# Making the two parts of 48 weight tiles with a casting transfer, a ScalarE multiplication and an adding transfer

## The chip, the cores and the metric

The kernel runs on one core of one Trainium2 chip. The metric is the device time of one execution in microseconds (us); lower is better. The kernel before was timed three times: 2293.43, 2293.59 and 2295.14 us, median 2293.59.

## What is computed

Four layers of a small language model run one after the other on 512 tokens of width 1024, all in float32: a gated linear recurrence, an attention with forget gates, and twice a hybrid layer (the "second block"). Only the hybrid layer's short convolution is touched by the change. Cut to that, the reference is:

```python
def hybrid_layer(x, positions, ...):
    h = rmsnorm(x, norm_mix)
    proj = h @ w_in                                  # w_in: 1024 x 9216
    cb, cc, cu, q, k, v, g, ga, gb = jnp.split(proj, split_points, axis=-1)
    z = conv(cc * cu)                                # depthwise, 3 taps
    y_conv = (cb * z) @ w_conv_out
    y_ret = retention_mixer(q, k, v, g, ...)
    merged = jax.nn.sigmoid(ga) * y_conv + jax.nn.sigmoid(gb) * y_ret
    x = x + merged @ w_o
    h2 = rmsnorm(x, norm_mlp)
    return x + jnp.square(jax.nn.relu(h2 @ w_up)) @ w_down
```

cb, cc and cu are 1024 wide each, so each layer has 3 x 8 output tiles of 128 features, and the two layers have 48.

## The kernel before

Activations lie with features on the 128 partitions and the 512 tokens along the free side. Every matrix product is done three times on parts of its operands: a float32 value is split into a high part in TensorE's reduced format (float32r) and a low part that holds the rest, and the products high x high, high x low and low x high are added up in PSUM. These are the three matmuls of `mm3`, lines 254, 255 and 256. One projection, `proj`, takes one weight tile of 128 x 1024 (eight blocks of 128 x 128) through 24 matmuls on 512 columns and gives one output tile of 128 features.

The class `Stream` makes the weight tiles in the order of their use. For each it loads the raw tile on SP's queue (512 KB), lets ScalarE cast it into the high part `wh` (line 59) and VectorE subtract that from the raw tile into the low part `wl` (line 60). Raw tiles have four buffers, high and low parts three each. A call of `next` sets going the work on tiles up to two ahead. As there are three buffers, tile i+3 can be written only when the last matmul that reads tile i is over: line 255 is the last reader of `wh`, line 256 that of `wl`.

In the convolution stage of a layer the loop runs over eight output tiles j. For each j it projects cb, cc and cu in this order (`cb_0`, `cc_0`, `cu_0`, `cb_1` and so on); VectorE empties each PSUM tile (lines 1089, 1092, 1095), applies the taps (1096, 1098), multiplies (1099), and splits the outcome into `zH` and `zL` with ScalarE (269, 270). GpSimd does little there: `rr`, the square of the row factor (1080), and two small fills (1085). The stage before it multiplies by `w_ret_out` (tiles `wr_0` to `wr_7`), the one behind it projects the gates `ga`.

TensorE's order is that of the program. The other engines' order is set by a scheduler that runs over the whole program; each engine and each queue then goes through its list strictly in order, and waits where an operand or a buffer isn't ready.

Of the kernel before, what the change touches and what calls it, by code (L numbers as in the profile page):

```python
# [7 lines left out]
F32 = mybir.dt.float32  # L8
F32R = mybir.dt.float32r
# [20 lines left out]

# columns of the packed per-partition vectors
VEC = {}
# [15 lines left out]
class Stream:  # L48
    """Weights in order of use: load, split into two float32r parts that add up exactly."""

    def __init__(self, tc, raw, hi, lo, items, ahead):
        self.nc, self.raw, self.hi, self.lo = tc.nc, raw, hi, lo
        self.items, self.ahead = items, ahead
        self.done, self.taken = [], 0
        self.sums = self.sraw = None
        self.pooled = 0  # so many of the next sums go to GpSimd, while VectorE has much else to do

# [4 lines left out]
    def _emit_sums(self, i, s1, s2):  # L62
        """Weights of two output tiles in Winograd's seven forms, each a pair of [P, 4, P] parts.

        Rows of the 2 x 2 blocks A are the output tiles, columns the halves of the contraction.
        """
        nc, hw, nh = self.nc, KD * P, KD * P // 2
        eng = nc.gpsimd if self.pooled > 0 else nc.vector
        self.pooled -= 1
        r1 = self.raw.tile([P, hw], F32, tag="wraw", name=f"wr{i}a")  # L70
        r2 = self.raw.tile([P, hw], F32, tag="wraw", name=f"wr{i}b")
        nc.sync.dma_start(r1, s1)
        nc.sync.dma_start(r2, s2)
        a11, a12, a21, a22 = r1[:, :nh], r1[:, nh:], r2[:, :nh], r2[:, nh:]
        out = {}

        def whole(names, src):
            h = self.hi.tile([P, hw], F32R, tag="whi", name=f"wh{i}{names[0]}")
            l = self.lo.tile([P, hw], F32R, tag="wlo", name=f"wl{i}{names[0]}")
            self._split(h, l, src)  # L80
            for n, nm in enumerate(names):
                c = slice(n * nh, (n + 1) * nh)
                out[nm] = tuple(t[:, c].rearrange("p (a b) -> p a b", b=P) for t in (h, l))

        def half(nm, src):
            h = self.sums.tile([P, nh], F32R, tag="shi", name=f"sh{i}{nm}")
            l = self.sums.tile([P, nh], F32R, tag="slo", name=f"sl{i}{nm}")
            self._split(h, l, src)
            out[nm] = tuple(t.rearrange("p (a b) -> p a b", b=P) for t in (h, l))

        def sraw(nm):
            return self.sraw.tile([P, nh], F32, tag="sraw", name=f"sr{i}{nm}")

        whole(("A11", "A12"), r1)
        v1 = sraw("S1")
        eng.tensor_add(v1, a21, a22)
        half("S1", v1)
        eng.tensor_sub(a21, a11, a21)
        whole(("S3", "A22"), r2)
        v2 = sraw("S2")  # L100
        eng.tensor_sub(v2, v1, a11)
        half("S2", v2)
        v4 = sraw("S4")
        eng.tensor_sub(v4, a12, v2)
        half("S4", v4)
        self.done.append(out)

    def _emit(self):
        nc = self.nc
        src, a, b = self.items[len(self.done)]  # L110
        if a is None:
            return self._emit_sums(len(self.done), src, b)
        n = a * b
        i = len(self.done)
        r = self.raw.tile([P, KD * P], F32, tag="wraw", name=f"wr{i}")
        h = self.hi.tile([P, KD * P], F32R, tag="whi", name=f"wh{i}")
        l = self.lo.tile([P, KD * P], F32R, tag="wlo", name=f"wl{i}")
        for c in range(0, n, n if i else n // 4):
            cs = slice(c, c + (n if i else n // 4))
            nc.sync.dma_start(r[:, cs], src[:, cs])  # L120
            self._split(h[:, cs], l[:, cs], r[:, cs])
        self.done.append(
            (h[:, :n].rearrange("p (a b) -> p a b", a=a), l[:, :n].rearrange("p (a b) -> p a b", a=a))
        )
# [16 lines left out]
class Map:  # L141
    """A pool whose tags stand for tags of other pools."""

# [8 lines left out]
def build(tc, A, out, dbg=None):  # L152
# [3 lines left out]
    with ctx:  # L156
# [11 lines left out]

# [1 line left out]
        items = []  # L170

# [30 lines left out]
        for l in range(2):  # L202
# [11 lines left out]
            for j in range(8):  # L214
                for t in range(3):
                    add(f"w_in{l}", 8 * t + j, KD, P)
            add(f"w_in{l}", 48, KD, P)
# [6 lines left out]
            for g in range(4):  # L224
                for f in range(0, 8, 2):
                    items.append((A[f"w_up{l}"][8 * g + f], None, A[f"w_up{l}"][8 * g + f + 1]))
                for j in range(8):
                    add(f"w_down{l}", 8 * g + j, KD, P)
        W = Stream(tc, wraw, whi, wlo, items, 2)

# [1 line left out]
        vec = cst.tile([P, NVEC], F32, name="vec")  # L232
# [38 lines left out]

# [1 line left out]
        def rsqrt_row(dst, src, scale, tp, tag, load=True):  # L273
            """dst = 1 / sqrt(src * scale + EPS), all float32 of one shape: a first value and a Newton step."""
            shape = [P, src.shape[-1]]
# [11 lines left out]
        def colsum(acc, tp, tag):  # L287
            """Sum of acc over its partitions, on every partition of a PSUM tile."""
            h = tp.tile([P, S], F32R, tag="cs_h", name=f"csh_{tag}")
# [7 lines left out]
        class Norm:  # L297
            """Splits x * gain as tiles of x come, and sums their squares."""

# [38 lines left out]
        class PairNorm:  # L338
            """As Norm, with Winograd's forms of x * gain: blocks are halves of the features by halves of the tokens."""

# [26 lines left out]
        def pair(tag, forms, cp, cs, first=False):  # L367
            """Two output tiles [P, S] by Winograd's variant of Strassen's product."""
            w = W.next()
# [47 lines left out]
        def columns(r, tag):  # L417
            """[P, 4]: the row r with tokens on partitions."""
            ps = psum(f"rc_{tag}")
# [6 lines left out]
        def log1p_small(dst, e, tp, shape, tag):  # L426
            """log(1 + e) for e in [0, 1], to float32 accuracy in relative terms."""
            d = tp.tile(shape, F32, tag="lp_d", name=f"lpd_{tag}")
# [14 lines left out]
        def trig():  # L443
            """cos and sin of position * frequency, [frequency twice, token]: sin on partitions ..63, cos on 64.. first."""
            pos, kk, ang = sind.bitcast(I32), sind, cosd
# [21 lines left out]
            act.copy(cosd[:64], cosd[64:])  # L467
            # rows 64.. multiply the second half into the first one
            act.mul(sind[64:], sind[:64], -1.0)

        # =====================================================================
        # layer 1: LRU
        # =====================================================================
        with ExitStack() as lc:
# [12 lines left out]

            # softplus(-a_param), times -4 and -8
            sp = cst.tile([P, 12], F32, name="sp")
# [130 lines left out]

        # =====================================================================
        # layer 2: forgetting attention
        # =====================================================================
        with ExitStack() as lc:
# [19 lines left out]

            # keys: high parts twice; low parts, and over the other half of the rows the cumulated forget gates
            k1 = t1.tile([P, 2, S], F32R, name="k1")
# [4 lines left out]
            def fox_forget(ft):  # L651
                """Log sigmoid of the forget gates, [token, block of tokens and head], in two parts."""
                fa, fe = (t2.tile([P, 64], F32, tag="pr1", name=n) for n in ("fa", "fe"))
# [17 lines left out]

            # P^T of a head, key block kb from column 384 * kb + query on
            PTW = 3 * 384 + S
# [185 lines left out]

        # =====================================================================  # L860
        # second block
        # =====================================================================
        def finish(ah, nrm, tp):
            """Last output tiles by halves of the tokens, with the last norm of one half beside the products of the other."""
            S2, JS = S // 2, (5, 6, 7)
# [58 lines left out]
        for li in range(2):  # L924
# [3 lines left out]
            with ExitStack() as lc:  # L928
# [24 lines left out]
                def first_rows():  # L953
                    """1 / rms of the layer's input, and what follows from it."""
                    if li:
                        r = nrm.rows(tn)
                    else:
                        # final norm of the first block and first norm of the second, in one
                        r0 = nrm.rows(tn)
# [221 lines left out]

# [1 line left out]
def lay_out(inputs):  # L1183
# [98 lines left out]
```

## Time and profile before

| | |
|---|---|
| median of three runs | 2293.59 us |
| profiled execution, span from first to last instruction | 2293.6 us |
| TensorE matmuls, busy | 2238.3 us, 98% |
| VectorE, busy | 1543.9 us, 67% |
| ScalarE, busy | 1065.4 us, 46% |
| GpSimd, busy | 369.0 us, 16% |
| moved by DMA | 210.42 MB, 92 GB/s on average |
| mean granted TensorE clock | 0.991 |

The profiled execution has no other time on its page than its span, which equals the median of the runs. Matmul durations overlap in the profile, since they are pipelined; how fast they follow one another is read from their starts. Line numbers in this part are those of the kernel before. In the changed kernel the code from `mm3` on stands 14 lines further down, and the cast and subtraction of `Stream` stand in lines 60 and 61.

### The profile page before, as it was taken

What the parts mean: (1) busy time and instruction counts of PE and PEld (TensorE: products, weight loads), DVE (VectorE), ACT (ScalarE), POOL (GpSimd) and SP (SyncE); (2) the same over time, 40 slices, a digit from 0 to 9 for tenths busy, and PEclk for the clock granted to TensorE, in tenths of its full rate; (3) what the DMA queues carried; (4) which work ended last, traced back from release to release, by engine and by line L of the source; (5) the groups of instructions that cost most, each with busy time, mean ns of one, the idle gap of its engine ahead of it and who ended that gap; (6) DMA issues with size and microseconds to landing.
All of it is one profiled execution on the core that took longest, in us unless ns stands there. A gap on an engine that the chain in (4) does not pass through costs nothing.

```text
span 2293.6 us, 30071 instructions
## 1 busy us (share of the span) xinstructions
PE 2238.3 (98%) x11818; PEld 1909.7 (83%) x11818; DVE 1543.9 (67%) x2256; ACT 1065.4 (46%) x1629; POOL 369.0 (16%) x269
## 2 busy tenths in 40 slices
PE   8898999999999999999999999999999999999998
PEld 6687778887888888887998998988888887998996
DVE  7987877777776445448875774766345548875774
ACT  5666577765556222235543444556222225443443
POOL 3434211113211000003310112211000004210112
PEclk9999999999999999999999999999999999999999
DMA  4133222222222332332332333222333322333331
GB/s 153 64 99 97 90 65 74 65 74 80 81 94 74 101 100 94 98 95 74 110 102 95 100 109 99 89 89 80 96 97 95 98 92 83 101 103 100 97 107 55
DMA packets 62509, 210.42 MB, mean 92 GB/s; under 512 B 6944, under 2 KB 11424, under 8 KB 62368
## 3 DMA queue, kind: packets, MB, share of 16 engines
q1 hardware_dynamic: 59552, 204.43, 28.1%
q10 hardware_dynamic: 2672, 3.81, 0.6%
q8 instruction: 93, 1.52, 0.3%
q14 instruction: 48, 0.39, 0.1%
q0 software_dynamic: 144, 0.26, 0.0%
HBM read 206.37 MB, written 2.10 MB: 91 GB/s over the span
## 4 chain that ended last, share of the span: by engine, by line
PE 82%; DVE 5%; ACT 1%; issue 1%; POOL 0%; DVEq 0%; ACTq 0%; POOLq 0%
PE dn L255 5%; PE dn L256 5%; PE dn L254 5%; PE up L255 4%; PE up L256 4%; PE up L254 4%; PE ro L981 1%; PE wr L256 1%; PE wc L254 1%; PE wc L256 1%; PE wc L255 1%; PE wr L255 1%; PE wr L254 1%; PE ga L254 1%; PE ga L256 1%
## 5 line engine op out<-in xcount | busy, mean ns | idle before, releaser
L59 ACT CAST wh<-wr 128x1024 fp32r<-128x1024 f32 (+2 forms) x332 | 337.2, 1017 | 707.9 <-PE dn L255 120.5
L60 DVE TENSOR_TENSOR wl<-wr,wh 128x1024 fp32r<-128x1024 f32 (+2 forms) x332 | 398.5, 1202 | 49.7 <-ACT wh L59 47.9
L255 PE MATMUL dn<-aL,wh 128*128 128x512 f32 x488 | 192.9, 395 | 0.3 <-DVE aL L270 0.3
L256 PE MATMUL dn<-aH,wl 128*128 128x512 f32 x488 | 192.8, 395 | 0.0
L254 PE MATMUL dn<-aH,wh 128*128 128x512 f32 x488 | 192.7, 395 | 0.0
L399 POOL TENSOR_TENSOR s_up<-s_up,sz_up 128x256 f32<-128x256 f32 x32 | 52.6, 1644 | 473.5 <-DVE sz_up L398 163.8
L1169 DVE TENSOR_TENSOR x<-dn,x 128x512 f32<-128x512 f32 x61 | 42.0, 689 | 111.1 <-PE dn L256 110.8
L255 PEld LDWEIGHTS dn<-aL,wh 128*128 128x128 f32 x488 | 91.5, 187 | 22.7 <-DVE aL L270 0.7
L256 PEld LDWEIGHTS dn<-aH,wl 128*128 128x128 f32 x488 | 91.5, 187 | 22.3
L254 PEld LDWEIGHTS dn<-aH,wh 128*128 128x128 f32 x488 | 91.5, 187 | 22.1
L326 POOL TENSOR_TENSOR nacc_m<-nacc_m,nsq_m 128x512 f32<-128x512 f32 x14 | 21.0, 1499 | 486.4 <-ACT nsq_m L325 486.4
L256 PE MATMUL rv<-wh,xL 128*128 128x256 f32 x256 | 72.4, 283 | 0.0
L255 PE MATMUL rv<-wl,xH 128*128 128x256 f32 x256 | 72.4, 283 | 0.0
L254 PE MATMUL rv<-wh,xH 128*128 128x256 f32 x256 | 72.4, 283 | 0.0
L1151 ACT ACTIVATE c_up<-c_up 128x512 f32<-128x512 f32 x64 | 40.5, 633 | 35.0 <-DVE c_up L1150 34.7
L254 PE MATMUL wo<-mH,wh 128*128 128x512 f32 x128 | 51.1, 399 | 0.0
L256 PE MATMUL wr<-yrH,wl 128*128 128x512 f32 x128 | 51.1, 399 | 0.0
L254 PE MATMUL wc<-zH,wh 128*128 128x512 f32 x128 | 50.6, 396 | 0.0
L256 PE MATMUL wc<-zH,wl 128*128 128x512 f32 x128 | 50.6, 395 | 0.0
L255 PE MATMUL wc<-zL,wh 128*128 128x512 f32 x128 | 50.5, 395 | 0.0
L255 PE MATMUL wr<-yrL,wh 128*128 128x512 f32 x128 | 50.5, 394 | 0.0
L256 PE MATMUL wo<-mH,wl 128*128 128x512 f32 x128 | 50.4, 394 | 0.0
(1561 smaller groups left out, 7144.5 us busy)
## 6 DMA issues: line engine op xcount, KB each, us to landing
wr<-in_w_in SPq DMA_DIRECT2D x112, 512.0 KB, 3.5
wr<-in_w_down SPq DMA_DIRECT2D x64, 512.0 KB, 3.5
wr<-in_fox_w_in SPq DMA_DIRECT2D x24, 512.0 KB, 3.5
wr<-in_lru_w_in SPq DMA_DIRECT2D x23, 512.0 KB, 3.6
wr<-in_w_v SPq DMA_DIRECT2D x16, 512.0 KB, 3.5
wr<-in_w_ret_out SPq DMA_DIRECT2D x16, 512.0 KB, 3.5
wr<-in_w_conv_out SPq DMA_DIRECT2D x16, 512.0 KB, 3.6
wr<-in_w_o SPq DMA_DIRECT2D x16, 512.0 KB, 3.5
```

What stands on the lines that cost most here:

```text
L59: self.nc.scalar.copy(h, src)
L60: self.nc.vector.tensor_sub(l, src, h.bitcast(F32))
L254: pe.matmul(ps, wH, aH, start=start, stop=False)
L255: pe.matmul(ps, wH, aL, start=False, stop=False)
L256: pe.matmul(ps, wL, aH, start=False, stop=stop)
L326: (dve if j > 5 and acc is self.acc2 else pool).tensor_add(acc, acc, sq)
L399: pool.tensor_add(s5, s5, z)
L981: pe.matmul(po[i][:, q0:], vp[:, kb, vs], sp_[:, so], start=n == 0, stop=n == 11)
L1151: act.activation(t, t, AF.Square)
L1169: dve.tensor_add(x[:, j], ps, x[:, j])
```

## The change

The 48 weight tiles of cb, cc and cu (24 in each layer) are made in another way; all others stay as they were. A set `by_dma` holds their places in the order of weights. For these, a transfer on GpSimd's queue casts the weights from memory straight into `wh`; ScalarE writes -`wh` into `wl`; and a second transfer on GpSimd's queue, with addition, adds the weights from memory to `wl`. The raw tile, its load on SP's queue and VectorE's subtraction fall away for them. Each of these weight tiles is read from memory twice.

```diff
@@ class Stream, _emit
         n = a * b
         i = len(self.done)
+        if i in self.by_dma:
+
+            h = self.hi.tile([P, KD * P], F32R, tag="whi", name=f"wh{i}")
+            l = self.lo.tile([P, KD * P], F32R, tag="wlo", name=f"wl{i}")
+            nc.gpsimd.dma_start(h[:, :n], src)
+            nc.scalar.mul(l[:, :n], h[:, :n].bitcast(F32), -1.0)
+            nc.gpsimd.dma_start(l[:, :n], src, accum_op=mybir.AluOpType.add)
+            self.done.append(
+                (h[:, :n].rearrange("p (a b) -> p a b", a=a), l[:, :n].rearrange("p (a b) -> p a b", a=a))
+            )
+            return
         r = self.raw.tile([P, KD * P], F32, tag="wraw", name=f"wr{i}")
@@ build
             for j in range(8):
                 for t in range(3):
+                    by_dma.add(len(items))
                     add(f"w_in{l}", 8 * t + j, KD, P)
...
         W = Stream(tc, wraw, whi, wlo, items, 2)
+        W.by_dma = by_dma
```

The rest of the diff takes comments out. TensorE's list is the same as before. In the lists below, `wh129` is the high part of weight tile 129, `wl129` its low part; tiles 129, 130, 131 are those of cb_0, cc_0, cu_0 of the first layer, 132 to 134 those of cb_1, cc_1, cu_1, and so on. In brackets stand the engines and queues that an instruction waits for (DMASW: GpSimd's transfers, DMAHW: those of the other queues).

GpSimd's list of the kernel before, from the last sum of the retention heads over the convolution stage to the first sum of squares behind it:

```order
L986 TENSOR_TENSOR gacc0_3_6664<-gacc0_3_6664,gsq0_3_6665 128x512 [waits DVE_49,Activation_49]
L1080 TENSOR_TENSOR rr_7201<-r_b_5201 128x512 [waits DMAHW5_49,DMAHW3_49,DMAHW6_49,DVE_49,DMAHW7_49,PE_49,Pool_49]
L1085 MEMSET zp0_7205 128x2
L1085 MEMSET zp1_7206 128x2
L326 TENSOR_TENSOR nacc_m0_8597<-nacc_m0_8597,nsq_m0_4_8676 128x512 [waits Activation_49]
```

There were three instructions in the whole stage. GpSimd's list of the changed kernel from the same place, where the stage begins:

```order
L1000 TENSOR_TENSOR gacc0_3_6664<-gacc0_3_6664,gsq0_3_6665 128x512 [waits DVE_49,Activation_49]
L120 DMA wh129_7126<-in_w_in0 128x1024 [waits DVE_49,PE_49]
L122 DMA wl129_7127<-in_w_in0 128x1024 [waits Activation_49]
L120 DMA wh130_7157<-in_w_in0 128x1024 [waits DVE_49,PE_49]
L122 DMA wl130_7158<-in_w_in0 128x1024 [waits Activation_49]
L120 DMA wh131_7208<-in_w_in0 128x1024 [waits DVE_49,PE_49]
L1094 TENSOR_TENSOR rr_7199<-r_b_5201 128x512 [waits DMAHW5_49,DMAHW6_49,DMAHW3_49,DMAHW7_49,PE_49,Pool_49]
```

Five transfers now stand between the heads' last sum and `rr`. The same list some rows further on, for the tiles of cb_1 to cc_2:

```order
L120 DMA wh132_7240<-in_w_in0 128x1024 [waits DMASW1_49,PE_49]
L122 DMA wl131_7209<-in_w_in0 128x1024 [waits Activation_49]
L122 DMA wl132_7241<-in_w_in0 128x1024 [waits DMASW2_49,Activation_49]
L120 DMA wh133_7272<-in_w_in0 128x1024 [waits DMASW3_49,PE_49]
L122 DMA wl133_7273<-in_w_in0 128x1024 [waits DMASW4_49,Activation_49]
L120 DMA wh134_7309<-in_w_in0 128x1024 [waits DMASW5_49,PE_49]
L120 DMA wh135_7341<-in_w_in0 128x1024 [waits DMASW6_49,PE_49]
L122 DMA wl134_7310<-in_w_in0 128x1024 [waits DMASW7_49,Activation_49]
L122 DMA wl135_7342<-in_w_in0 128x1024 [waits DMASW0_49,Activation_49]
L120 DMA wh136_7373<-in_w_in0 128x1024 [waits DMASW1_49,PE_49]
L122 DMA wl136_7374<-in_w_in0 128x1024 [waits DMASW2_49,Activation_49]
```

From here on a pattern of six rows repeats to the end of the stage: the casting transfers of a cu tile and of the cb tile behind it (134, 135), their two adding transfers, then the casting and the adding transfer of a cc tile (136). The adding transfer of a cu tile (`wl134`) has moved behind the casting transfer of the next cb tile (`wh135`), which waits for TensorE to give a buffer free. `wl131`, of cu_0, stands behind `wh132` in the same way.

## Rows read from the trace of the kernel before

**Rows 1.** The page: busy time by engine, and the chain by engine.

```profile
PE 2238.3 (98%) x11818; PEld 1909.7 (83%) x11818; DVE 1543.9 (67%) x2256; ACT 1065.4 (46%) x1629; POOL 369.0 (16%) x269
...
PE 82%; DVE 5%; ACT 1%; issue 1%; POOL 0%; DVEq 0%; ACTq 0%; POOLq 0%
```

**Rows 2.** Busy time by windows: the conv projections of both layers.

```profile
core 0: us, PE busy (x) PEld busy (x) DVE busy (x) ACT busy (x) POOL busy (x), PEclk, DMA share, GB/s
811.70:942.20 130.50, 130.50 (x577) 108.08 (x576) 67.22 (x83) 29.66 (x31) 1.11 (x3) 1.00 0.30 97
1675.40:1805.00 129.60, 129.60 (x573) 107.33 (x572) 69.53 (x87) 29.44 (x31) 0.00 (x0) 1.00 0.31 96
```

**Rows 3.** Tiles cb and cc: evacuations, min/median/max ns, first to last start.

```profile
L1089 DVE TENSOR_TENSOR cb<-cb,r_b x8: 691/692/692, 817.4 to 931.6; 128x512 f32<-128x512 f32 x8
...
L1092 DVE TENSOR_TENSOR cc<-cc,rr x16: 691/692/692, 822.9 to 1795.1; 128x512 f32<-128x512 f32 x16
```

**Rows 4.** Timeline of ScalarE, 811 to 823: start, length, idle before and releaser.

```profile
811.66 1.05 ACT L59 CAST wh<-wr 128x1024 fp32r<-128x1024 f32 x1 [4.55 <-PE wr L255]
...
822.59 1.06 ACT L59 CAST wh<-wr 128x1024 fp32r<-128x1024 f32 x1 [4.38 <-PE cc L255]
```

**Rows 5.** Timeline of all engines where the stage begins.

```profile
811.70 0.40 PE L254 MATMUL cb<-xH,wh 128*128 128x512 f32 x1
...
811.93 0.19 PEld L256 LDWEIGHTS cb<-xH,wl 128*128 128x128 f32 x1
...
812.00 1.04 POOL L1080 TENSOR_TENSOR rr<-r_b 128x512 f32<-128x512 f32 x1 [81.54 <-PE wr L256]
```

**Rows 6.** Groups by line in that window: busy us, mean ns, idle before.

```profile
L60 DVE TENSOR_TENSOR wl<-wr,wh 128x1024 fp32r<-128x1024 f32 x24 | 29.5, 1227 | 1.9 <-ACT wh L59 1.8
L59 ACT CAST wh<-wr 128x1024 fp32r<-128x1024 f32 x24 | 25.4, 1056 | 75.3 <-PE cc L255 35.1 <-PE cu L255 30.7 <-PE wr L255 4.6
```

**Rows 7.** DMA queues (packets, MB, share) and issues (KB each, us to landing).

```profile
q1 hardware_dynamic: 59552, 204.43, 28.1%
...
q0 software_dynamic: 144, 0.26, 0.0%
...
wr<-in_w_in SPq DMA_DIRECT2D x112, 512.0 KB, 3.5
...
wr<-in_fox_vf SPq DMA_DIRECT2D x1, 272.0 KB, 2.7
...
tri<-in_tri POOLq DMA_DIRECT2D x1, 256.0 KB, 3.2
```

**Rows 8.** Timeline of GpSimd around its one transfer.

```profile
263.51 0.74 POOL L643 DMA_DIRECT2D tri<-in_tri  x1 [0.31 <-POOL nacc_n L326]
264.30 0.52 POOL L648 MEMSET k<- 64x512 f32 x1
```

**Rows 9.** Timeline of TensorE where it idled: in brackets the idle time before.

```profile
289.85 0.74 PE L666 MATMUL cum<-tri,fH 128*16 128x512 f32 x4 [1.06 <-issue]
...
596.09 0.50 PE L254 MATMUL rs<-rqH,rkH 128*128 128x512 f32 x1 [1.57 <-ACT rkH L269]
```

**Rows 10.** Windows behind these, TensorE alone: length, busy, granted clock, DMA share, GB/s.

```profile
core 0: us, PE busy (x), PEclk, DMA share, GB/s
596.96:600.37 3.41, 3.41 (x12) 0.50 0.21 70
287.00:292.00 5.00, 3.94 (x21) 1.00 0.36 108
```

**Rows 11.** Timeline of TensorE at the lower clock.

```profile
564.06 0.63 PE L254 MATMUL rk<-xH,wh 128*128 128x512 f32 x1
564.49 0.63 PE L255 MATMUL rk<-xL,wh 128*128 128x512 f32 x1
564.91 0.63 PE L256 MATMUL rk<-xH,wl 128*128 128x512 f32 x1
```

**Rows 12.** Timeline of TensorE in the stage before.

```profile
807.96 0.40 PE L256 MATMUL wr<-yrH,wl 128*128 128x512 f32 x1
808.20 0.39 PE L254 MATMUL wr<-yrH,wh 128*128 128x512 f32 x1
808.43 0.39 PE L255 MATMUL wr<-yrL,wh 128*128 128x512 f32 x1
808.66 0.40 PE L256 MATMUL wr<-yrH,wl 128*128 128x512 f32 x1
```

More of the change, by code (lines that the diff above doesn't have):

```diff
@@ L55, in __init__ @@
         self.sums = self.sraw = None
+        self.by_dma = set()
         self.pooled = 0
@@ L167, in psum @@
             return psp.tile([P, S], F32, tag="ps", name=name)
-        items = []
+        items, by_dma = [], set()
         def add(name, idx, a, b):
```

## The prediction

> **What bounds the kernel now.** I read the busy table first: TensorE is busy 98% of the span, VectorE 67%, and the chain that ended last lies 82% on TensorE [rows 1]. The change touches 48 weight tiles, in one stage that comes twice (the projections cb, cc, cu of the two layers of the second block), so I then read the stage by windows: TensorE is busy 130.50 of 130.50 us in the first and 129.60 of 129.60 in the second [rows 2]. It waits for nothing there. VectorE works 67 of 130 us off the path; taking work from it can give nothing back in this stage. So the question is only whether the new way of making a weight tile is always done in time.
>
> Three distances decide that. One projection (24 matmuls on one weight tile): the evacuations of cb run from 817.4 to 931.6 us for eight outputs [rows 3], 114.2 us over 21 projections, 5.44 us each. When a buffer comes free: a pool holds three tiles, so tile i+3 goes where tile i was; before, ScalarE's cast starts at 811.66, 822.59 and so on, each time as the last L255 matmul of an older tile ends [rows 4]. From that event the next tile's low part is wanted 0.27 us later, by the weight load at 811.93 [rows 5]. Today the raw tile has long been loaded by then, and cast and subtraction take 1.06 + 1.23 us [rows 6] of two projections' 10.9 us.
>
> **The change part by part.** Removed in each stage: 24 loads on SP's queue, 24 casts (1.06 us) and 24 subtractions (29.5 us of VectorE) [rows 6]: worth 0, since TensorE waits for none of them. Added on ScalarE: 24 multiplications of the casts' shape. I take the cast's 1.06 us; no row has this one, but ScalarE is busy only 29.66 of 130.5 us [rows 2], so double would be hidden as well. The two zp fills and rr on GpSimd now stand behind a load; rr ran at 812.00 [rows 5] and its first reader is the evacuation of cc at 822.9 [rows 3]: nothing. SP's later loads start earlier, into raw buffers that the 48 tiles no longer use: nothing.
>
> What counts is the new chain, per tile: buffer free, casting load on GpSimd's queue, multiplication, adding load on the same queue. GpSimd takes its instructions in order, and the new order puts the adding load of each cu tile behind the casting load of the next cb tile, which waits until the projection two ahead of that cu has ended (the order is shown with the change). So cu's adding load has one projection, 5.44 us, plus the 0.27: 5.71 us.
>
> Prices. A casting load: the one that the trace has on GpSimd's queue, 256 KB, took 0.74 us to issue [rows 8] and 3.2 to land; on SP's queue 272 KB took 2.7 and 512 KB 3.5 [rows 7], so 512 KB cast is 3.2 + 0.85 = 4.05 us. How much of that is data: SP's queue moved 204.43 MB in 28.1% of 16 engines' span [rows 7], 0.281 x 2293.6 = 644.5 us with all 16, or 644.5 x 0.524 / 204.43 = 1.65 us per tile. Lead-in and landing are the other 2.4.
>
> An adding load is nowhere in the trace. Low end: it costs what a casting load does and does not feel the one before it: 0.79 us for the issue ahead (263.51 to 264.30) [rows 8] + 4.05 = 4.84 us, 0.87 inside the limit; nothing is lost, and nothing gained. In the queue's order, behind the other's data: 2.4 + 1.65 + 1.65 = 5.70, just at the limit. If it has to fetch two inputs, the weights and the tile it adds to, its data takes 3.3: 2.4 + 1.65 + 3.3 = 7.35 us, 1.64 late. High end: twice that data time again, 6.6 (rival below). I take the two inputs: the nearest row prices one tile moved once, and an addition must read one more tile than a copy.
>
> The Trainium skill, "Collectives: The Full Stack", under "The bandwidth ceiling: the fold count and why AG ≠ RS ≠ AR", says that an adding transfer is slower not for its adding but for its second read on the same ring, measured at 1.93 to 1. No run here shows it yet; by it the data would take 3.2 us, and the lateness would be 1.54 instead of 1.64.
>
> How often: cu_0 to cu_6 in each stage (cu_7 has no load of this kind behind it), and once per stage cc_0, whose casting load queues behind the first adding load in the same way: 16 waits x 1.64 = 26 us. In steady state the queue carries 3 x (1.65 + 3.3) = 14.85 us per three projections of 16.31: it keeps up, with little to spare.
>
> The clock comes on top. After TensorE idled 1.57 us at 596.09 its granted clock was 0.50, the lower of its two levels (1.2 of 2.4 GHz), from 596.96 to 600.37; after an idle 1.06 us at 289.85 it stayed at 1.00 [rows 9, 10]. At the lower level matmuls come 0.425 us apart (564.06, 564.49, 564.91) [rows 11] instead of 5.44 / 24 = 0.227, so 3.41 us hold 8 instead of 15 and cost 8 x 0.198 = 1.6 us. A wait of 1.64 lies just past the one that had this effect, so I charge it to half of them: 8 x 1.6 = 13 us. Sum: 26 + 13 = +39. The profiled span, 2293.6, is the median shown (2293.59), so no correction: 2333 us.
>
> **Rivals.**
> No wait (not slower). The addition costs one read, or the two loads of a pair overlap: 4.84 to 5.70 us, and up to 5.71 it decides. TensorE runs on and the time stays at 2293 to 2297. For it: both numbers come from rows, and only the adding itself is guessed. Against it: at 5.70 there is no reserve left for the hop to GpSimd. The Trainium skill's page "DMA: Bandwidth & Descriptors", under "Anatomy of one DMA — SWDGE (gpsimd) path", would have it so: 2.0 us plus bytes over 436 GB/s, that is 2.0 + 1.2 + 1.2 = 4.4 us for the pair, and 5.6 with a second read. The one row disagrees: its fit gives 2.6 us for 256 KB, and the trace has 3.2.
>
> The queue becomes the bound. If the adding load's data takes over 3.8 us, three tiles need more than the 16.31 us of their projections (3 x (1.65 + 3.8) = 16.35), and each further us costs 3 per group of three. At 6.6 us: 3 x 8.25 = 24.75, 8.4 late, in 16 groups 135 us: 2429. For it: an addition into a tile must read, add and write back. Against it: the transfer engines were busy only 30% of this stage [rows 2].
>
> Faster. Matmuls come 0.227 us apart in cb and about 0.233 in the stage before (807.96, 808.20, 808.43, 808.66) [rows 12], so something moves this by 2 to 3%; if it is VectorE's traffic, its loss could give up to 2% of 260 us, 5 us: 2288. Nothing ties the two.
>
> **How the numbers follow.** Forecast with waits of about 0.3 to 3 us per group: 0.5, by itself 2300 to 2370. No wait: 0.2. Queue bound: 0.27. Faster: 0.03. The measurement can tell 0.2% (4.6 us) from no change. So slower 0.77, same 0.2, faster 0.03. The range goes from just below no change, 2291, to 2425, where the queue's data time is 6.5 us; beyond lies about a tenth.
>
> **What would show it.** In the profile after: GpSimd's queue up from 144 packets to 144 + 96 x 144 = 13968 and from 0.26 to about 50.6 MB; TensorE idle before matmuls of cu on the low part, seven per stage, released by a transfer, 1 to 3 us each; each stage 17 to 22 us longer than 130 and nothing else moved; clock 0.50 after the longer waits. I am wrong if cu never waits (then adding loads land within 5.7 us of their pair's start), or if cb and cc wait as often as cu (then the queue is the bound).

## The result, and the profile after

The changed kernel takes 2355.52 us in the median (2354.69 to 2358.24, four runs) against 2294.36 for the kernel before, measured beside it: a ratio of 1.0266, 95% interval 1.0252 to 1.0281. It is 61 us slower; the forecast was 39 us slower. The profiled execution took 2354.69 us and spans 2352.9.

The page of the changed kernel, in the order of [rows 1, 7]: busy time by engine, the DMA queues, the chain by engine.

```profile
PE 2262.7 (96%) x11818; PEld 1920.8 (82%) x11818; DVE 1489.1 (63%) x2208; ACT 1065.2 (45%) x1629; POOL 442.4 (19%) x365
...
q1 hardware_dynamic: 52640, 179.26, 23.1%
q0 software_dynamic: 13968, 50.60, 9.4%
...
PE 71%; issue 11%; DVE 4%; POOL 3%; ACT 1%; DMA 1%; POOLq 0%; DVEq 0%; ACTq 0%
```

GpSimd's queue (q0) holds the 13968 packets and 50.6 MB that were forecast. VectorE is relieved of 55 us, which buys nothing: TensorE's share of the chain falls from 82% to 71%.

The same stages as in [rows 2], from the first matmul of cb_0 to the first of ga_0:

```profile
core 0: us, PE busy (x) PEld busy (x) DVE busy (x) ACT busy (x) POOL busy (x), PEclk, DMA share, GB/s
809.20:972.20 163.00, 143.37 (x578) 114.19 (x577) 42.68 (x61) 30.75 (x33) 33.26 (x48) 0.94 0.67 152
1699.60:1859.40 159.80, 141.81 (x577) 113.01 (x576) 42.77 (x61) 30.73 (x32) 33.59 (x48) 0.95 0.67 155
```

Before, by the starts of the same matmuls, each took 130.6 us. (The second window of [rows 2] begins 5.7 us behind the first matmul of its stage, which changes nothing in its reading: no wait lies in the 130.6 us either.) The two are 32.4 and 29.2 us longer, 61.6 in all; everything else in the program keeps its time to within 2.5 us. So the whole loss lies in the stage that the change touches. What TensorE waits for there (engine, line, releaser: total, times, longest):

```profile
PE cu L270 <- DMA wl<-in_w_in: 32.2, 16, 2.9
...
PE cc L270 <- DMA wl<-in_w_in: 5.4, 4, 3.2
```

All waits are for the low part, released by the adding load: 37.6 us in 20 waits, 16 of them, 32.2 us, in front of cu. The granted clock over the two stages is 0.94 and 0.95. With two levels, 1.00 and 0.50, that is 12% and 10% of the stages at the lower one, 35.5 us (the trace has eleven stretches at 0.50 there, of 3.4 us each), in which matmuls come 0.425 us apart instead of 0.227 [rows 11]: 35.5 x (1 - 0.227/0.425) = 16.5 us. A wait also costs some 0.3 us beyond its length: the projection of cu that starts at 863.72 waits 1.69 us, stays at a clock of 1.00 and takes 7.43 us, where 5.44 + 1.69 would be 7.13. About half of this is the overlap of two matmuls that is lost (0.39 us long, 0.227 apart). 20 x 0.3 = 6 us. That makes 60 of 61.6; the rest was not followed.

The loads on GpSimd's queue (size, median us to landing), where [rows 7] had one of 256 KB:

```profile
wh<-in_w_in POOLq DMA_DIRECT2D x48, 512.0 KB, 6.0
wl<-in_w_in POOLq DMA_DIRECT2D x48, 512.0 KB, 5.3
```

The adding load is near what was reckoned for its lead-in, data and landing (2.4 + 3.3 = 5.7). The casting load is not: 6.0 instead of 4.05. GpSimd's timeline over one group of three projections shows why (start, length, idle before and releaser):

```profile
843.87 0.86 POOL L122 DMA_DIRECT2D wl<-in_w_in  x1 [2.18 <-ACT wl L121]
844.43 0.86 POOL L120 DMA_DIRECT2D wh<-in_w_in  x1
852.05 0.86 POOL L122 DMA_DIRECT2D wl<-in_w_in  x1 [6.76 <-ACT wl L121]
853.08 0.56 POOL L120 DMA_DIRECT2D wh<-in_w_in  x1 [0.17 <-PE cu L270]
858.52 0.53 POOL L120 DMA_DIRECT2D wh<-in_w_in  x1 [4.88 <-PE cb L270]
860.52 0.89 POOL L122 DMA_DIRECT2D wl<-in_w_in  x1 [1.46 <-ACT wl L121]
863.65 0.86 POOL L122 DMA_DIRECT2D wl<-in_w_in  x1 [2.25 <-ACT wl L121]
864.20 0.88 POOL L120 DMA_DIRECT2D wh<-in_w_in  x1
```

ScalarE's timeline beside it, its multiplications only:

```profile
850.70 1.06 ACT L121 ACTIVATE wl<-wh 128x1024 fp32r<-128x1024 f32 x1 [7.13 <-DMA wh<-in_w_in]
...
859.16 1.06 ACT L121 ACTIVATE wl<-wh 128x1024 fp32r<-128x1024 f32 x1 [1.87 <-DMA wh<-in_w_in]
862.29 1.06 ACT L121 ACTIVATE wl<-wh 128x1024 fp32r<-128x1024 f32 x1 [2.07 <-DMA wh<-in_w_in]
```

Read them together. At 844.43 the casting load of a cc tile is issued, right behind two adding loads. The multiplication that waits for it starts at 850.70, 6.3 us later. Until the multiplication of that tile is over, GpSimd's list has nothing to issue: 6.76 us idle, released by ScalarE. The next cu tile's casting load goes out at 853.08, behind that cc tile's adding load; its multiplication starts at 859.16; its adding load is issued at 860.52 and not, as the prediction had it, when the cb tile's casting load (858.52) is out of the way: GpSimd waits 1.46 us longer, for the multiplication. The matmul that needs this low part starts at 866.03, 7.5 us after the cb tile's casting load was issued; the prediction had 7.35 from there. So at this place the route that was forecast and the tile's own late casting load end almost together. The next group of the pattern begins at 864.20, 19.8 us after 844.43, where three projections take 16.3.

The transfer engines are not full in this time (windows, all engines; DMA share is the second number from the end):

```profile
844.00:850.50 6.50, 4.52 (x13) 3.45 (x13) 0.43 (x1) 0.00 (x0) 1.29 (x2) 0.74 0.92 208
850.50:853.50 3.00, 3.00 (x15) 2.48 (x14) 0.46 (x1) 1.06 (x1) 1.28 (x2) 1.00 0.00 0
853.50:858.70 5.20, 5.20 (x24) 4.32 (x23) 3.83 (x7) 0.62 (x1) 0.32 (x2) 1.00 0.92 202
```

Nearly full, 3 us at 0.00, nearly full: the queue stands empty while the multiplication and the next issue are under way.

### The profile page after: what moved, and what is told of

Its sections match the earlier page's. It is cut to its first block, busy times and chain, and to the rows that moved or that the text cites. A ratio compares the mean times of both kernels' runs of the same rounds, so it can differ in the third digit from the quotient of the medians.

```text
span 2352.9 us, 30124 instructions
## 1 busy us (share of the span) xinstructions
PE 2262.7 (96%) x11818; PEld 1920.8 (82%) x11818; DVE 1489.1 (63%) x2208; ACT 1065.2 (45%) x1629; POOL 442.4 (19%) x365
## 3 DMA queue, kind: packets, MB, share of 16 engines
q0 software_dynamic: 13968, 50.60, 9.4%
## 4 chain that ended last, share of the span: by engine, by line
PE 71%; issue 11%; DVE 4%; POOL 3%; ACT 1%; DMA 1%; POOLq 0%; DVEq 0%; ACTq 0%
PE dn L270 5%; PE dn L269 5%; PE dn L268 5%; PE up L269 4%; PE up L270 4%; PE up L268 4%; POOL wl L122 1%; PE ro L995 1%; PE wc L268 1%; PE wc L270 1%; PE wc L269 1%; PE ga L268 1%; PE ga L270 1%; PE gb L268 1%; PE gb L270 1%
## 5 line engine op out<-in xcount | busy, mean ns | idle before, releaser
L60 ACT CAST wh<-wr 128x1024 fp32r<-128x1024 f32 (+1 forms) x284 | 286.4, 1010 | 547.3 <-PE dn L269 120.3
L61 DVE TENSOR_TENSOR wl<-wr,wh 128x1024 fp32r<-128x1024 f32 (+1 forms) x284 | 341.4, 1204 | 48.1 <-ACT wh L60 45.9
L121 ACT ACTIVATE wl<-wh 128x1024 fp32r<-128x1024 f32 x48 | 50.9, 1061 | 207.1 <-DMA wh<-in_w_in 198.6
L1109 DVE TENSOR_TENSOR zp<-cu,cc 128x512 f32<-128x512 f32 x16 | 11.1, 692 | 126.1 <-PE cu L270 126.1
L270 PE MATMUL cu<-xH,wl 128*128 128x512 f32 x128 | 58.2, 454 | 32.2 <-DMA wl<-in_w_in 32.2
L122 POOL DMA_DIRECT2D wl<-in_w_in x48 | 42.0, 876 | 193.1 <-ACT wl L121 191.2
L120 POOL DMA_DIRECT2D wh<-in_w_in x48 | 33.3, 694 | 202.2 <-PE wr L270 140.6
L270 PEld LDWEIGHTS cu<-xH,wl 128*128 128x128 f32 x128 | 28.0, 219 | 45.1 <-DMA wl<-in_w_in 38.9
L1106 DVE TENSOR_TENSOR cc<-cc,rr 128x512 f32<-128x512 f32 x16 | 11.1, 691 | 78.9 <-PE cc L270 78.9
L269 PE MATMUL cu<-xL,wh 128*128 128x512 f32 x128 | 56.5, 442 | 0.0
```

Of the source, the lines that this page charges most:

```text
L60: self.nc.scalar.copy(h, src)
L61: self.nc.vector.tensor_sub(l, src, h.bitcast(F32))
L120: nc.gpsimd.dma_start(h[:, :n], src)
L121: nc.scalar.mul(l[:, :n], h[:, :n].bitcast(F32), -1.0)
L122: nc.gpsimd.dma_start(l[:, :n], src, accum_op=mybir.AluOpType.add)
L269: pe.matmul(ps, wH, aL, start=False, stop=False)
```

## The experiments

Each kernel was timed in three rounds beside the kernel before (medians of before 2294.2 to 2295.6). Two theories stood at the start. Lead time: the chain of a tile is longer than the time that three buffers leave. Order: the adding load of cu is held up in GpSimd's list behind a casting load that waits for a buffer. The rival to both was the queue's rate.

**Program order** (e_order; its edit in short). Each casting load is put behind the adding load of the tile before it.

```diff
-            nc.gpsimd.dma_start(h[:, :n], src)
+            with tc.issue_after(previous_adding_load):
+                nc.gpsimd.dma_start(h[:, :n], src)
```

> The changed kernel with GpSimd's list put into the program's order: each casting load behind the adding load of the tile before it, so that no adding load stands behind a casting load that waits for a buffer. Order theory (the prediction's words: the adding load of cu is late because it stands behind the casting load of the next cb): cu's waits go, 2294 to 2315 us. Lead-time theory (what makes the chain long is that each load's data comes behind that of the load before it): now every casting load comes behind an adding load, and a tile takes 2.4 + 2.6 to 3.3 + 1.4 to 1.65 + multiplication and hops 1.3 = 7.7 to 8.6 us of the queue's loop against 5.44: cb, cc and cu all wait, 48 x 2.3 to 3.2 us; 2400 to 2450 us.

2422.14 us, ratio 1.0549 (1.0531 to 1.0566). The order theory as a sole cause is refuted: with no adding load behind a waiting casting load all three projections wait (16 of cu, 16 of cc, 14 of cb). That the old order costs nothing in the changed kernel is not shown by this, since the new one also puts every casting load behind an adding load. GpSimd now takes 8.1 us per tile, always released by the multiplication:

```profile
864.25 0.88 POOL L126 DMA_DIRECT2D wl<-in_w_in  x1 [6.54 <-ACT wl L125]
864.80 0.88 POOL L124 DMA_DIRECT2D wh<-in_w_in  x1
872.32 0.88 POOL L126 DMA_DIRECT2D wl<-in_w_in  x1 [6.64 <-ACT wl L125]
```

The estimate was 7.7 to 8.6: casting load behind an adding load, then the multiplication, then the next adding load, with nothing overlapping.

**A fourth buffer** (e_own4). The first three tiles of a stage stay where they were, the other 21 rotate through four buffers of a pool in memory that the stage does not use otherwise; tiles are asked for three ahead. The edit, here in short, also gives `mH` and `mL`, which the stage behind this one fills, another pool.

```diff
+            own = i - 3 in self.by_dma
-            h = self.hi.tile([P, KD * P], F32R, tag="whi", name=f"wh{i}")
+            h = (self.own if own else self.hi).tile(..., tag="oh" if own else "whi", ...)
```

> The changed kernel with one buffer more for the 48 tiles: the first three tiles of a stage use the old three buffers, the other 21 rotate through four of their own (in memory that the stage does not use otherwise), and tiles are asked for three ahead. Same loads, multiplications and order pattern. Lead-time theory (the chain of casting load, multiplication and adding load takes some 12.9 us through one queue, while three buffers leave 10.9 + 0.27; its data, some 4.6 us per tile, fits into the 5.44 us of a projection): with 16.3 us of lead the waits of cu_1 to cu_7 go, those of cc_0 and cu_0 at the start of a stage stay, about 3 to 6 us per stage; 2300 to 2315 us. Rate theory (GpSimd's queue carries a tile in no less than 6.8 us, a third of the 20.3 us per three projections seen): the waits stay whatever the lead; 2345 to 2360 us.

2340.42 us, 1.0194 (1.0179 to 1.0209): between the two expectations, so neither theory holds alone. The trace shows both at work one after the other. Tiles 4 to 12 of a stage never wait: the extra lead is used up over them. From then on the cb tiles, a third of the projections, wait 0.2 to 2.3 us. In the first stage GpSimd's list from then on repeats every 18.8 us per three tiles, and TensorE is no longer among its releasers:

```profile
892.31 0.86 POOL L122 DMA_DIRECT2D wl<-in_w_in  x1 [7.92 <-ACT wl L121]
892.86 1.43 POOL L120 DMA_DIRECT2D wh<-in_w_in  x2
900.45 0.89 POOL L122 DMA_DIRECT2D wl<-in_w_in  x1 [6.16 <-ACT wl L121]
901.66 0.89 POOL L122 DMA_DIRECT2D wl<-in_w_in  x1 [0.33 <-ACT wl L121]
902.21 0.90 POOL L120 DMA_DIRECT2D wh<-in_w_in  x1
911.11 0.86 POOL L122 DMA_DIRECT2D wl<-in_w_in  x1 [8.00 <-ACT wl L121]
```

So there is a third cause, a loop in the list itself: twice per group an adding load stands at its head waiting for its own casting load to come through the queue, and nothing else can be issued.

**The addition left out** (e_plain2). The second load casts and overwrites; the low parts are then the weights themselves.

```diff
-            nc.gpsimd.dma_start(l[:, :n], src, accum_op=mybir.AluOpType.add)
+            nc.gpsimd.dma_start(l[:, :n], src)
```

> The changed kernel with the second load as a plain casting load, without addition (the low parts then hold the weights themselves). Same number of loads, same order, same waits. Two-reads theory (an adding load's data takes nearly twice that of a casting load): per tile the queue carries 3.0 to 3.3 us instead of 4.0 to 4.6, the chain shortens by 1.2 to 1.6 us for its own load and as much for the adding load ahead of its casting load; at most cu_0 and cc_0 wait a little; 2294 to 2305 us. Rival (the lateness comes from the hops between GpSimd, queue and ScalarE, not from the data): waits of 1 to 2 us stay at all cu; 2325 to 2350 us.

2306.77 us, 1.0051 (1.0036 to 1.0066). Just above the expected range: eight waits of cu remain, 5.5 us in all, and no lower clock in the stages. As many loads and hops, but 49 us less: most of the loss comes from the data of the adding loads. The queue's share prices it. Here and in the next kernel:

```profile
q0 software_dynamic: 13968, 50.60, 6.8%
```

0.068 x 2302.8 us of span = 156.6 us for 96 casting loads, 1.63 each (the prediction had 1.65). In the changed kernel 0.094 x 2352.9 = 221 us for 48 of each kind: 4.6 per tile, so 2.98 for an adding load, 1.83 times a casting one.

**Only the adding load** (e_scalar_cast): the raw tile is loaded by SP's queue and cast by ScalarE as before.

```diff
-            nc.gpsimd.dma_start(h[:, :n], src)
+            r = self.raw.tile([P, KD * P], F32, tag="wraw", name=f"wr{i}")
+            nc.sync.dma_start(r[:, :n], src)
+            nc.scalar.copy(h[:, :n], r[:, :n])
```

> One part of the change alone: the raw tile is loaded on SP's queue and cast by ScalarE as in the kernel before; the low part comes from ScalarE's multiplication and GpSimd's adding load; VectorE is left out. From the free buffer: cast 1.06 + multiplication 1.06 + adding load 5.3 and hops = about 7.7 us against 11.15: no waits by the lead-time theory, 2293 to 2299 us. Rival (the adding load as such is too slow): 16 waits of cu stay, above 2320 us.

2294.28 us against 2294.18, ratio 1.0002 (0.9992 to 1.0011): no wait in either stage. The share of its queue is

```profile
q0 software_dynamic: 7056, 25.43, 6.5%
```

0.065 x 2291.1 / 48 = 3.10 us per adding load, beside the 2.98 above. The adding load by itself costs nothing here; VectorE is relieved just as in the change.

**Only the casting load** (e_cast_dve): the low part is VectorE's subtraction from a raw tile.

```diff
-            nc.scalar.mul(l[:, :n], h[:, :n].bitcast(F32), -1.0)
-            nc.gpsimd.dma_start(l[:, :n], src, accum_op=mybir.AluOpType.add)
+            r = self.raw.tile([P, KD * P], F32, tag="wraw", name=f"wr{i}")
+            nc.sync.dma_start(r[:, :n], src)
+            nc.vector.tensor_sub(l[:, :n], r[:, :n], h[:, :n].bitcast(F32))
```

> The other part alone: the casting load on GpSimd's queue makes the high part, and the low part is VectorE's subtraction from a raw tile that SP's queue loads; no multiplication, no adding load. From the free buffer: 4.05 + 1.23 and hops = 5.6 us against 11.15: no waits by the lead-time theory, 2293 to 2299 us. Rival (any load on GpSimd's queue that waits for a buffer is too late): waits at cu; above 2305 us.

2295.02 us, 0.9998 (0.9988 to 1.0007): as the lead-time theory has it.

**The change for cu alone** (e_cu_only).

```diff
-                    by_dma.add(len(items))
+                    if t == 2:
+                        by_dma.add(len(items))
```

> The change for the 16 cu tiles alone; cb and cc are made as in the kernel before. The same chain, three buffers, but a queue that is empty when the chain begins. Queueing theory: casting load 4.05, multiplication and hops 1.4, adding load 2.4 + 3.0 = 10.85 us against 11.15: no waits, or under 0.5 us each; 2293 to 2301 us. Rival (the chain is too long by itself, queue or not): 16 waits of 1 us or more remain; 2315 to 2335 us.

2295.46 us, 0.9999 (0.9990 to 1.0009). The same chain with three buffers fits if the queue is empty. Its loads land in

```profile
wh<-in_w_in POOLq DMA_DIRECT2D x16, 512.0 KB, 3.8
wl<-in_w_in POOLq DMA_DIRECT2D x16, 512.0 KB, 5.3
```

so 3.8 + 5.3 + 1.4 for the multiplication and hops = 10.5 us of 11.15. In the full change the casting load lands 2.2 us later (6.0), which breaks this limit by itself. But no casting load of cb stands ahead of cu's adding load here either: this run takes away the queueing and the order together, and cannot weigh one against the other.

**Casting one tile ahead of adding, everywhere** (e_pipe, four own buffers; e_pipe3, the three old ones). The adding load of tile i is held back until the casting load of tile i+1 has been issued, but for the first two of a stage (the edit in short):

```diff
             nc.gpsimd.dma_start(h[:, :n], src)
             nc.scalar.mul(l[:, :n], h[:, :n].bitcast(F32), -1.0)
-            nc.gpsimd.dma_start(l[:, :n], src, accum_op=mybir.AluOpType.add)
+            add_the_tile_before()          # its adding load, next in GpSimd's list
```

> The four own buffers of e_own4, and GpSimd's list with each adding load behind the casting load of the next tile for all tiles (cast i+1, add i, cast i+2, add i+1, ...) instead of the pattern of six. Turnaround theory (in e_own4 the buffers no longer bind, but the list does: in each group of three it issues a casting load, then nothing until that load has landed behind two adding loads and has been multiplied, so the queue stands idle for some 4 us of the group): with a casting load always issued ahead of an adding load the loop takes about 0.6 + 1.63 + 3.0 = 5.2 us of a projection's 5.44; only the start of a stage waits, 3 to 6 us; 2297 to 2312 us. Rate theory (the queue cannot carry a tile in less than about 6 us): waits of about 2 us per three projections stay; 2335 to 2350 us.

2324.43 us, 1.0115 (1.0100 to 1.0130), above the expected range. After the start of a stage the expectation holds: tiles 5 to 24 of each stage never wait, and GpSimd's casting loads are released by TensorE, not by ScalarE:

```profile
860.95 0.92 POOL L113 DMA_DIRECT2D wl<-in_w_in  x1
866.04 0.55 POOL L134 DMA_DIRECT2D wh<-in_w_in  x1 [4.17 <-PE cc L291]
866.57 0.92 POOL L113 DMA_DIRECT2D wl<-in_w_in  x1
871.66 0.55 POOL L134 DMA_DIRECT2D wh<-in_w_in  x1 [4.17 <-PE cu L291]
```

What the range had left out: the start costs 4 to 5 us of waits and 1.6 us of lower clock per stage, and a projection takes 5.62 us here instead of 5.44, as 866.04 to 871.66 shows. The two stages are 11.0 and 10.3 us longer than before; the other 7 to 8 of the 29 us lie outside them, and were not followed.

> The list order of e_pipe with the changed kernel's three buffers. Now every adding load stands behind a casting load that waits for the projection two ahead, as the prediction had it for cu alone: landing 2.4 + 1.63 + 3.0 = 7.0 us after that, against 5.71: by the lead-time theory every projection waits, 46 x 1.3 = 60 us, and the clock on top where a wait passes 1.5; 2345 to 2400 us. If the order alone were the cause (and not order and buffers together), this kernel would be near e_pipe, under 2315 us.

2373.35 us, 1.0338 (1.0314 to 1.0362). This is the mechanism that the prediction put forward, made for every tile: 32 waits, 54 us. In the steady part GpSimd waits for TensorE at the casting load and issues the adding load right behind it, with no wait for a multiplication:

```profile
886.91 0.55 POOL L134 DMA_DIRECT2D wh<-in_w_in  x1 [6.13 <-PE cb L287]
887.44 0.92 POOL L113 DMA_DIRECT2D wl<-in_w_in  x1
...
wl<-in_w_in POOLq DMA_DIRECT2D x48, 512.0 KB, 7.6
```

The adding load is issued 0.53 us after the casting load and lands 7.6 after that, 8.1 in all, where 7.0 were expected. So the forecast order makes a tile late without any late multiplication. Order and buffers are needed together; either alone (e_own4, e_pipe3) still waits.

**The rest of e_pipe** (e_pace, e_pipe21). e_pace uses the buffers of e_own4 for tiles made as before; e_pipe21 is e_pipe with the first three tiles of a stage made as before, and every adding load held back.

```diff
 # e_pace: in place of the two loads and the multiplication
+            nc.sync.dma_start(r[:, :n], src)
+            self._split(h[:, :n], l[:, :n], r[:, :n])
 # e_pipe21
-                    by_dma.add(len(items))
+                    if j:
+                        by_dma.add(len(items))
```

> The buffers of e_own4 without the change: all tiles are loaded, cast and subtracted as in the kernel before, but 21 of the 24 tiles of each conv stage lie in the four own buffers. In e_own4 and e_pipe a projection from these buffers took 5.62 us, from the ordinary ones 5.44. Place theory (the pace of the matmuls depends on where the weight tiles lie, not on how they were made): 5.62 again, 42 x 0.18 = 8 us; 2300 to 2304 us. Load theory (GpSimd's transfers slow the matmuls): 5.44, 2293 to 2297 us.

> e_pipe with the first three tiles of each stage (cb_0, cc_0, cu_0) made as in the kernel before, so that only 42 tiles go the new way, in the four own buffers and with the list of e_pipe. Turnaround theory: the loop keeps up (5.2 us of 5.44 to 5.62), and without the start of the stage no wait is left at all; what stays is the pace of these buffers: 2300 to 2306 us. If waits of 1 us or more stay (above 2310 us), the queue's rate is a bound of its own even with this order.

e_pace takes 2306.97 us, 1.0053 (1.0038 to 1.0068), and e_pipe21 2307.07, 1.0056 (1.0039 to 1.0073): the same time. They are 3 and 1 us above their ranges. In both traces a stage takes 134.4 us, 3.8 more than before, and the two together 7.7; some 5 us more are lost outside them. Of these, 3.0 us in e_pace and 2.8 in e_pipe21 are waits of the `up` product (`h2 @ w_up`) for a low part that VectorE makes (`sl180S`, `sl316S`), which the kernel before does not have; whether the moved `mH` and `mL` cause them was not tried. The first stage of e_pipe21:

```profile
810.30:944.70 134.40, 134.40 (x577) 108.42 (x576) 44.50 (x63) 29.86 (x32) 30.14 (x42) 1.00 0.80 180
```

TensorE is busy 134.40 of 134.40 us, clock 1.00. So 42 of the 48 tiles can be made by the two loads without one wait; what it costs there is the buffers, not the loads. No kernel here beats the one before: TensorE waits for nothing in these stages there, so relieving VectorE has nothing to give back. e_scalar_cast is the one that relieves it at no cost.

## Why the prediction was right, and where its sizes were off

- The number: 2355.52 lies in the stated range, but that range (2291 to 2425) holds the rival without waits as well, and 61 us are half as much again as the 39. What speaks for the forecast is where the waits are and what releases them; the stages became 32.4 and 29.2 us longer, not 17 to 22.
- That the stage was bound by TensorE alone, and that VectorE's relief would give back nothing: right (e_scalar_cast, ratio 1.0002 with VectorE's subtractions gone).
- That the new chain would be late at cu and not at cb: right in the main, 16 of 20 waits at cu; the four others are at cc, two at the starts of the stages, as forecast, and two small ones later. cu_7 waits too, 1.2 and 0.6 us, which was excluded: its casting load comes late without any load of cb behind it.
- The price of the adding load: data 2.98 to 3.10 us against 3.3, landing 5.3 against 5.7. Right within a tenth. The Trainium skill, "Collectives: The Full Stack", under "The bandwidth ceiling: the fold count and why AG ≠ RS ≠ AR", has 1.93 to 1 for a step with two source reads against a copy; this queue shows 1.83. The skill's other rule cited, in "DMA: Bandwidth & Descriptors" under "Anatomy of one DMA — SWDGE (gpsimd) path", gives an estimate of 3.2 us for 512 KB; alone on its queue the casting load took 3.8 (e_cu_only), again 0.6 more.
- The order, cu's adding load behind cb's casting load: it is there, and enough by itself (e_pipe3), but it was priced too low. 7.35 us were reckoned from the one load's issue to the other's landing; e_pipe3 has 8.1, and in the changed kernel, by the starts in the timelines, it is 7.3 to 8.8 us to the matmul that waited in 11 of the 14 groups of cu_0 to cu_6, against a limit of 5.8 (858.52 to 866.03, less the wait of 1.69). In the other three (cu_0 twice, cu_3 once) it is 9.4 to 12.2: there the multiplication ended last by far.
- The price of the casting load, 4.05 us, was wrong under load. It holds for an idle queue (3.8), but in the change most casting loads come behind an adding load, and took 6.0. This opens a second way to the same wait, which the prediction did not count: cu's own casting load is late, and GpSimd holds its adding load until the multiplication is over (1.46 us at 860.52). At cu_7 this way acts alone. In most groups both end so close together that how the surplus, 37.6 us of waits instead of 26, divides between them stays open.
- "The queue carries 14.85 us per 16.31: it keeps up." The data was right (13.8), the conclusion wrong: the in-order list leaves the queue empty for part of each group (3 us in the one shown; DMA share 0.67 over the stages), and the list's own loop takes 18.8 us with buffers to spare (e_own4). Only with each casting load issued ahead (e_pipe, e_pipe21) does it keep up.
- The clock: 16.5 us against 13. Eight drops were charged; eleven came, six and five, behind waits of 1.98 to 3.17 us; the waits were longer than supposed.
- The rivals: no wait would have needed the addition to cost one read, and it costs 1.83 times that; even without the addition eight waits of up to 1.0 us are left (e_plain2); the bound by the queue's rate was not reached, or e_pipe21 would have waited; a faster TensorE without VectorE's traffic is refuted by e_scalar_cast.

## What to carry to other kernels

Where a tile goes through one in-order queue twice with a step on another engine in between, the load's price on an idle queue is not enough: write down what stands ahead of each issue in the list, and whose data is ahead of it in the queue, for a whole period, and compare that period with the consumer's. To make such a chain keep up, issue the first load of the next tile before the second load of this one, and give it the buffer that this needs; one of the two without the other did not do. And before an engine is relieved, ask whether it is waited for at all.

## What the runs showed of the hardware that was not expected

The pace of the same 24 matmuls changed with the place of their weight tiles. Within e_pace the first three projections of a stage, from the ordinary buffers, take 5.44 us and those behind them, from the own pool, 5.62, at a clock of 1.00, with the loads of the kernel before; with those of the change it is the same (e_pipe21). In e_pace's timeline matmuls come about 0.234 us apart, as they do in the stage of [rows 12]:

```profile
900.29 0.39 PE L272 MATMUL cc<-xH,wh 128*128 128x512 f32 x1
900.52 0.40 PE L273 MATMUL cc<-xL,wh 128*128 128x512 f32 x1
900.76 0.40 PE L274 MATMUL cc<-xH,wl 128*128 128x512 f32 x1
900.99 0.39 PE L272 MATMUL cc<-xH,wh 128*128 128x512 f32 x1
```

In the stage of [rows 12] the weight tiles lie in the ordinary buffers, and the moving tiles are others (`yrH`, `yrL`). So the place of the weight tiles does not settle the pace alone. What does was not tried.

The idle time before a stretch does not alone settle its clock. Three waits of cu in the changed kernel, and the windows behind them (TensorE alone: busy, granted clock, DMA share, GB/s):

```profile
846.13 0.59 PE L270 MATMUL cu<-xH,wl 128*128 128x512 f32 x1 [1.98 <-DMA wl<-in_w_in]
...
866.03 0.50 PE L270 MATMUL cu<-xH,wl 128*128 128x512 f32 x1 [1.69 <-DMA wl<-in_w_in]
...
1754.75 0.50 PE L270 MATMUL cu<-xH,wl 128*128 128x512 f32 x1 [2.27 <-DMA wl<-in_w_in]
```

```profile
846.40:849.80 3.40, 3.40 (x9) 0.50 1.01 270
866.30:869.70 3.40, 3.40 (x16) 1.00 1.00 263
1755.00:1758.40 3.40, 3.40 (x16) 1.00 0.95 252
```

After 1.98 us it fell to the lower of its two levels, after 1.69 and after 2.27 it did not, while before the change 1.57 us had been followed by it [rows 9, 10].
